# A branch projection computed by seven quarter products per pair of column blocks, and placed among the attention's projections

## The chip, the cores and the metric

The kernel runs on one core of a Trainium2 chip. The metric is the device time of one execution in microseconds (us); lower is better. A measurement is the median over several executions. One further execution was recorded by the hardware profiler, and the profile and the trace come from it.

The core has five engines that run side by side and meet through semaphores. TensorE (PE in the profile) multiplies matrices and writes its results to PSUM, eight banks of 128 x 512 float32. VectorE (DVE) and ScalarE (ACT) do elementwise work. GpSimd (POOL) and SyncE (SP) mainly issue transfers (DMA) here.

## What is computed

A decoder layer on 256 tokens of width 2048, all in float32:

```python
h = rms_norm(x, pre_norm_w)
proj = h @ w_in                       # q, k, v, z, beta, decay; mq, mk, mv, mz; gate_a, gate_b
oa = gated_delta_rule(...)            # 8 heads of 128, chunks of 64, then normed and gated
u_a = oa @ w_branch_a                 # 256 x 1024 @ 1024 x 2048
ob = moba_attention(...) * silu(mz)   # 8 heads of 128, causal
u_b = ob @ w_branch_b                 # 256 x 1024 @ 1024 x 2048
merged = sigmoid(gate_a) * u_a + sigmoid(gate_b) * u_b
x + rms_norm(merged @ w_out, post_norm_w)     # 256 x 2048 @ 2048 x 2048
```

## The kernel before

**Precision by halves.** A float32 number is held as a high and a low half of TensorE's faster float32 format. `split` (L211) makes both from a raw tile of weights: ScalarE casts the high half (L214), VectorE subtracts it from the raw tile to get the low one (L215). The pools of raw tiles, high halves and low halves have three buffers each. A product of two numbers is three matmuls: high by high, high by low, low by high.

**Projections.** `proj_n` (L347) computes 512 columns for both tiles of 128 tokens. For each 128 rows of the weights it issues six matmuls of 512 columns (three per token tile), and one split covers two such steps. `proj_t` (L329) computes 256 columns transposed, with eight steps of a 512- and a 256-column matmul per split. Weights come in raw tiles of 1 MB on SP's queue.

**The order of the work.** `ORDER` (L40) is the list of projection blocks in the order in which TensorE runs them: ga and gb are the column blocks of the two gates, mk a pair of attention heads (queries and keys, `attention`, L852), and so on. All small work is woven between the matmuls by queues of Python generators (`Queue`, L45). Each projection calls `tick` (L132) every step (in `proj_t`, every four steps), and a generator that yields a number n goes on 2n ticks later. So a tick is a place in TensorE's program. Blocks ga, gb and mk have 16 ticks each. A matmul stays in its place of the program; other engines' instructions get their order from a scheduler at build time, which takes a ready instruction that stands earlier in the program first.

**Queues that matter here.** `gq` carries the delta rule: its scores, the inverse, and `solve` (L695), which ends with `normed` (L731; tile so), then `yield OS_WAIT` and `turned_outputs` (L773; tile ot): these transpose the results and make the halves of oaT, the stationary operand of the first branch. `aq` carries, for each of two heads at a time, `attend` (L812) in four steps: scores and softmax (tile ms; VectorE L820 to L826), transposes (pp), values (po; VectorE's om, L841), transposes of the result (pt), from which halves of obT come (L849, L850). `halves` (L448) and the product with rrow (L859) finish the queries and keys.

**The branches and the end.** After the list, a loop over four column blocks (L962) computes `ua` (eight steps of `proj_n` on oaT), multiplies the gate ga by it (L965), computes `ub` on obT, multiplies gb (L968), and hands `merge` (L925) to a queue: it adds the two, transposes the sum (tile mt) and makes the halves of mT. 

The output projection then computes its first two column blocks for the first half of the rows by seven products instead of eight (the Winograd form of Strassen's scheme on 2 x 2 quarters: token tiles by halves of the 1024 rows, halves of the rows by column blocks). Sums of quarters of mT are formed by `merge` (sums_f, SH, SL), differences of weight quarters by `differences` (L917) from tiles tq that `load_quarter` (L908) fetches on POOL's queue. `product` (L986) is one product of two quarters: 12 matmuls, two splits, four ticks. Between the products stand `third(0)`, `third(1)` and `third(2)` (L1004), parts of another column block with 24 matmuls each on two splits. Two of the sums over products wait in a tile `kept` and are added at the end.

## Time and profile before

| | |
|---|---|
| median of 3 executions | 780.57 us (779.91 to 780.75) |
| the profiled execution's own time | 780.75 us |
| its span, first to last instruction | 778.8 us |
| matmuls on TensorE | 3947 |
| mean granted TensorE clock | 0.996 |
| moved by DMA | 149.24 MB, 192 GB/s on average |

How to read it: the rows of the page and of the trace give instructions as "line engine operation output<-input". A row of the chain of waits gives the start, the duration and what ran. Matmul durations overlap, so the pace is read from a stretch divided by its count. Tiles have the names of the program without their numbers: a_ua is the PSUM bank of the first branch, lo_mk a low half of mk's weights, tq a quarter for the differences.

### The profile page before, as it was taken

Reading aid. Unit: us, or ns where it says so; the run is one execution under the profiler, and the core shown is the slowest. Engines: PE = TensorE matmul, PEld = TensorE weight load, DVE = VectorE, ACT = ScalarE, POOL = GpSimd, SP = SyncE. Lnnn points to the kernel's source line nnn. Section 1 sums busy time; section 2 is a strip of 40 time slices with the busy share of each in tenths; the row PEclk is TensorE's granted clock in tenths of the full one; section 3 lists DMA queues with packets and bytes.
Section 4 is the critical chain, followed back from the end, with each engine's and each line's share of the span. In section 5 each row is a group of like instructions: output and inputs, shape, how many; then the busy total and the mean of one; then the engine's idle time right before and its main releaser. Section 6 shows DMA issues by size and latency. Waiting matters only on the chain.

```text
span 778.8 us, 10308 instructions
## 1 busy us (share of the span) xinstructions
PE 768.0 (99%) x3947; PEld 655.4 (84%) x3947; DVE 530.7 (68%) x876; ACT 412.1 (53%) x623; POOL 24.6 (3%) x47
## 2 busy tenths in 40 slices
PE   8999999999999999999999999999999999999996
PEld 7898988898888888888888888888888888888884
DVE  5787668887864898976444665555644668986673
ACT  5677665655565545455435647354454445465451
POOL 3000000010020000001100000000000000000000
PEclk9999999999999999999999999999999999999999
DMA  8576675467479555656943455555456555577442
GB/s 304 169 226 221 185 217 163 134 196 210 162 214 280 180 203 178 201 187 205 230 135 109 152 174 168 187 162 186 162 185 228 183 197 203 192 271 270 166 158 109
DMA packets 92823, 149.24 MB, mean 192 GB/s; under 512 B 3045, under 2 KB 46694, under 8 KB 92134
## 3 DMA queue, kind: packets, MB, share of 16 engines
q1 hardware_dynamic: 89958, 136.51, 54.4%
q0 software_dynamic: 2240, 11.02, 4.8%
q10 hardware_dynamic: 576, 1.05, 0.4%
q8 instruction: 31, 0.51, 0.3%
q14 instruction: 18, 0.15, 0.1%
HBM read 145.42 MB, written 3.15 MB: 191 GB/s over the span
## 4 chain that ended last, share of the span: by engine, by line
PE 95%; DVE 2%; ACT 2%; DMA 1%; issue 0%; SPq 0%; DVEq 0%
PE a_gb L140 11%; PE a_ga L140 11%; PE a_y L140 11%; PE a_k L140 6%; PE a_zg L140 6%; PE a_mq L140 6%; PE a_mk L140 6%; PE a_v L140 6%; PE a_zm L140 6%; PE a_mv L140 5%; PE a_ub L140 5%; PE a_ua L140 5%; PE a_q L140 4%; PE sv L140 2%; PE s L140 1%; PE po L140 1%
## 5 line engine op out<-in xcount | busy, mean ns | idle before, releaser
L140 PE MATMUL a_gb<-hi_gb,hT 128*128 128x512 f32 x256 | 83.2, 396 | 0.0
L140 PE MATMUL a_ga<-hi_ga,hT 128*128 128x512 f32 x256 | 80.7, 391 | 0.0
L215 DVE TENSOR_TENSOR lo_gb<-raw_gb,hi_gb 128x1024 fp32r<-128x1024 f32 x32 | 39.2, 1224 | 41.3 <-ACT hi_gb L214 41.3
L214 ACT CAST hi_gb<-raw_gb 128x1024 fp32r<-128x1024 f32 x32 | 33.7, 1052 | 49.2 <-PE a_gb L140 33.6
L140 PEld LDWEIGHTS a_ga<-hi_ga,hT 128*128 128x128 f32 x256 | 48.1, 188 | 9.9
L140 PEld LDWEIGHTS a_gb<-hi_gb,hT 128*128 128x128 f32 x256 | 48.1, 188 | 9.9
L214 ACT CAST hi_ga<-raw_ga 128x1024 fp32r<-128x1024 f32 x32 | 33.6, 1051 | 37.9 <-PE a_ga L140 28.0
L215 DVE TENSOR_TENSOR lo_ga<-raw_ga,hi_ga 128x1024 fp32r<-128x1024 f32 x32 | 39.1, 1223 | 16.6 <-ACT hi_ga L214 16.3
L140 PE MATMUL a_ga<-lo_ga,hT 128*128 128x512 f32 x128 | 49.9, 390 | 0.0
L140 PE MATMUL a_gb<-lo_gb,hT 128*128 128x512 f32 x128 | 49.8, 389 | 0.0
L140 PE MATMUL a_zg<-hi_zg,hT 128*128 128x348 f32 (+1 forms) x192 | 46.6, 322 | 0.0
L140 PE MATMUL a_mq<-hT,hi_mq 128*128 128x512 f32 x128 | 46.4, 405 | 0.0
L140 PE MATMUL a_mk<-hT,hi_mk 128*128 128x512 f32 x128 | 46.3, 403 | 0.0
L140 PE MATMUL a_y<-hi_y,mT 128*128 128x512 f32 x144 | 45.6, 390 | 0.0
L140 PE MATMUL a_v<-hT,hi_v 128*128 128x512 f32 x128 | 45.6, 399 | 0.0
L140 PE MATMUL a_q<-hT,hi_q 128*128 128x512 f32 x128 | 45.3, 395 | 0.0
L140 PE MATMUL a_ua<-hi_ua,oaT 128*128 128x512 f32 x128 | 41.8, 395 | 0.0
L140 PE MATMUL a_k<-hT,hi_k 128*128 128x512 f32 x128 | 41.1, 404 | 0.2 <-ACT hi_k L267 0.2
L140 PE MATMUL a_zm<-hi_zm,hT 128*128 128x512 f32 x128 | 40.6, 392 | 0.0
L140 PE MATMUL a_mv<-hi_mv,hT 128*128 128x512 f32 x128 | 40.1, 391 | 0.0
L140 PE MATMUL a_ub<-hi_ub,obT 128*128 128x512 f32 x128 | 40.0, 389 | 0.0
L140 PE MATMUL a_v<-hT,lo_v 128*128 128x256 f32 x128 | 35.9, 281 | 0.0
(318 smaller groups left out, 1905.0 us busy)
## 6 DMA issues: line engine op xcount, KB each, us to landing
raw_ga<-in_w_in_dram SPq DMA_DIRECT2D x16, 1024.0 KB, 5.0
raw_gb<-in_w_in_dram SPq DMA_DIRECT2D x16, 1024.0 KB, 5.1
raw_y<-in_w_out_dram SPq DMA_DIRECT2D x15, 1024.0 KB, 5.0
raw_q<-in_w_in_dram SPq DMA_DIRECT2D x8, 1024.0 KB, 5.6
raw_mv<-in_w_in_dram SPq DMA_DIRECT2D x8, 1024.0 KB, 5.1
raw_v<-in_w_in_dram SPq DMA_DIRECT2D x8, 1024.0 KB, 5.7
raw_zm<-in_w_in_dram SPq DMA_DIRECT2D x8, 1024.0 KB, 8.3
raw_mq<-in_w_in_dram SPq DMA_DIRECT2D x8, 1024.0 KB, 5.8
```

The source lines that it names most:

```text
L140: return pin(nc.tensor.matmul(*args, **kwargs))
L214: nc.scalar.copy(hi, raw)
L215: nc.vector.tensor_tensor(lo, raw, hi.bitcast(F32), op=ALU.subtract)
```

## The change

The first branch is computed for pairs of column blocks (0 and 1, then 2 and 3) by the same seven products as the output: token tile by half of oaT's rows on one side, half of the weights' rows by column block on the other. Each pair is one entry of the order, `ua0` and `ua1`; they stand before and after `mk3`. The second branch's blocks become a function `branch`: `ub0` and `ub1` stand in the order between gb1 and gb2, and blocks 2 and 3 run after the list with the merges. ga3 moves between mk1 and mk2, and gb0 and gb1 behind mk3 and ua1.

For this, the turned outputs are handled together: token tile 1 first, then tile 0, then four sums of quarters with halves of their own. The attention's queues stand still while these use all four auxiliary PSUM banks. Quarters of the first branch's weights are fetched on POOL's queue into the tiles of the delta rule and its gate as these come free; the pair's differences are spread on a queue of their own. Two rows of obT hold the fourth sum until both pairs are done.

The seven products become one function for both uses. It runs p5 first, then p1, copies c12 aside and c21 into c11 so that p2 and p6 add onto them, and adds the results in PSUM, without the tile `kept`. In the output projection two of the three parts `third` go ahead of the seven products, one stays between p6 and p2, and the differences are fetched and made after `ub1`.

```diff
+T_WAIT = 3
-OS_WAIT = 5
+OS_WAIT = 3
 ORDER = (
-    "q0 mv0 zg0 q1 kq2 kq3 zg1 v0 v1 v2 ga0 zm0 zm1 ga1 mv1 v3 ga2 ga3 mk0 mk1 gb0 mk2 gb1 mk3 gb2 gb3"
+    "q0 mv0 zg0 q1 kq2 kq3 zg1 v0 v1 v2 ga0 zm0 zm1 ga1 mv1 v3 ga2 mk0 mk1 ga3 mk2 ua0 mk3 ua1 gb0 gb1 ub0 ub1 gb2 gb3"
 ).split()
...
-        for q in (gq, vq, mq, *aq, *extra):
+        for q in (gq, vq, mq, *(() if held else aq), *extra):
             q.tick()
...
+    def fetch(tq, w, c, i):
+        rs, cs = (0, 512, 0)[i], (c + (1, 1, 0)[i]) * 512
+        nc.gpsimd.dma_start(tq[i], w[rs : rs + 512, cs : cs + 512].rearrange("(k p) c -> p k c", p=P))
+
+    def differences(tq, c, wait):
+        yield wait
+        for o, a, b in ((0, 0, 2), (1, 1, 0), (2, 1, 2)):
+            for u in range(2):
+                us = slice(2 * u, 2 * u + 2)
+                nc.vector.tensor_tensor(tq[o][:, us], tq[a][:, us], tq[b][:, us], op=ALU.subtract)
+                yield 1
+        formed.append(c)
...
+    def seven(quarter, s_, tq, w, c, banks, name, fill=lambda i: None, done=lambda b: None, more=lambda i: None):
+        c11, c12, c21, c22 = banks
+        product([s_[0]], tq[0], [c12], [True], f"{name}p5")
+        product([quarter(0, 0)], load(w, 0, c, name), [c21], [True], f"{name}p1")
+
+        s5 = tq[0][:, 0]
+        nc.scalar.copy(s5, c12)
+        nc.scalar.copy(c11, c21)
+        fill(0)
+        raw21 = load(w, 1, c, name)
+        product([s_[1]], tq[1], [c21], [False], f"{name}p6")
+        fill(1)
+        product([quarter(0, 1)], raw21, [c11], [False], f"{name}p2")
+        nc.vector.tensor_tensor(c12, c21, s5, op=ALU.add)
+        for u in range(2):
+            us = slice(2 * u, 2 * u + 2)
+            nc.vector.tensor_tensor(tq[1][:, us], raw21[:, us], tq[1][:, us], op=ALU.subtract)
+        product([s_[2]], tq[2], [c21], [False], f"{name}p7")
+        done(c11)
+        fill(2)
+        product([s_[3]], load(w, 1, c + 1, name), [c12], [False], f"{name}p3")
+        nc.vector.tensor_tensor(c22, c21, s5, op=ALU.add)
+        done(c12)
+        more(0)
+        more(2)
+        product([quarter(1, 1)], tq[1], [c21], [False], f"{name}p4")
+        more(1)
+        done(c22)
+        done(c21)
...
+    def branch_pair(i):
+        c = 2 * i
+        while not oas or c not in formed:
+            sq.tick()
+            gq.tick()
...
+        def done(b):
+            cc, t = place[id(b)]
+            nc.vector.tensor_tensor(ga[:, cc, t, :], ga[:, cc, t, :], b, op=ALU.mult)
+
+        def more(j):
+            if i == 0:
+                fetch(tua, wa, 2, j)
+
+        seven(quarters(oaT[0]), oas, tua, wa, c, (c11, c12, c21, c22), f"ua{c}", done=done, more=more)
+        pairs.append(i)
+        if i == 0:
+            sq.add(differences(tua, 2, 2))
...
-        def turned_outputs(t, oz):
...
+        def turned_outputs(ozs):
+            a = {}
+            for t in (1, 0):
+                for g in range(2):
+                    pt = aux_tile(f"ot_{t}_{g}")
+                    for hh in range(4):
+                        tr(pt[:, hh * P : (hh + 1) * P], ozs[t][:, g, hh, :], ident)
+                    a[t, g] = pt.rearrange("p (h n) -> p h n", n=P)
+                for g in range(2):
+                    ks = slice(4 * g, 4 * g + 4)
+                    halved(oT[:, ks, t * P : (t + 1) * P], oT[:, ks, S + t * P : S + (t + 1) * P], a[t, g])
+                yield 1
+            oa_f = big.tile([P, 2, 4, P], F32, tag="tv", name="oa_f")
+            x, y = (oa_f[:, i] for i in range(2))
+            nc.scalar.copy(x, a[1, 1])
+            nc.vector.tensor_tensor(a[1, 1], a[1, 0], x, op=ALU.add)
+            nc.scalar.copy(y, a[0, 0])
+            nc.vector.tensor_tensor(a[0, 0], a[1, 1], y, op=ALU.subtract)
+            nc.scalar.copy(x, a[0, 0])
+            yield 0.5
+            nc.vector.tensor_tensor(a[0, 1], a[0, 1], x, op=ALU.subtract)
+            nc.vector.tensor_tensor(a[1, 0], y, a[1, 0], op=ALU.subtract)
+            yield 0.5
+            sums = [None] * 3 + [tuple(ob_tile()[:, h, :].rearrange("p (k n) -> p k n", n=P) for h in (6, 7))]
+            for i, o, tag in ((0, (1, 1), "tt"), (1, (0, 0), "tw"), (3, (0, 1), None), (2, (1, 0), "tv")):
+                if tag:
+                    tl = big.tile([P, 2, 4, P], F32R, tag=tag, name=f"oas_{i}")
+                    sums[i] = tl[:, 0], tl[:, 1]
+                halved(*sums[i], a[o])
                 yield 0.5
+            oas.extend(sums)
...
+        obs.append(big.tile([P, H, 2 * S], F32R, tag="g0", name="obT"))
+        tg = big.tile([P, 2, 4, 512], F32, tag="g1", name="tq_g")
+        tz = big.tile([P, 4, 512], F32, tag="z2", name="tq_z")
+        tua.extend((tg[:, 0], tz, tg[:, 1]))
+        for i in (0, 2, 1):
+            fetch(tua, wa, 0, i)
+        sq.add(differences(tua, 0, T_WAIT))
         yield OS_WAIT
-        for t in range(NT):
-            yield from turned_outputs(t, ozs[t])
+        held.append(True)
+        yield from turned_outputs(ozs)
+        held.pop()
...
+    def branch(c):
+        for q in aq:
+            q.drain()
+        pb = proj_n(wb, c * 512, ob_tile(), H, f"ub{c}")
+        for t in range(NT):
+            nc.vector.tensor_tensor(gb_tile()[:, c, t, :], gb_tile()[:, c, t, :], pb[t], op=ALU.mult)
+        for t in range(NT):
+            nc.vector.tensor_tensor(ga[:, c, t, :], ga[:, c, t, :], gb_tile()[:, c, t, :], op=ALU.add)
+        if c == 1:
+            ty.extend(big.tile([P, 4, 512], F32, tag=f"z{i}", name=f"tq_{i}") for i in range(3))
+            for i in (0, 2, 1):
+                fetch(ty, wo, 0, i)
+            formed.clear()
+            sq.add(differences(ty, 0, T_WAIT))
...
-    for c in range(D // 512):
-        pa = proj_n(wa, c * 512, oaT[0], H, f"ua{c}")
-        for t in range(NT):
-            nc.vector.tensor_tensor(ga[:, c, t, :], ga[:, c, t, :], pa[t], op=ALU.mult)
-        pb = proj_n(wb, c * 512, ob_tile(), H, f"ub{c}")
-        for t in range(NT):
-            nc.vector.tensor_tensor(gb_tile()[:, c, t, :], gb_tile()[:, c, t, :], pb[t], op=ALU.mult)
-        mq.add(merge(c, 0.5 if c < 3 else 5))
...
+    mq.add(merge(0, 0.5))
+    mq.add(merge(1, 0.5))
+    branch(2)
+    mq.add(merge(2, 0.5))
+    branch(3)
+    mq.add(merge(3, 5))
...
+    third(0)
+    third(1)
+    while not formed or not summed:
         mq.tick()
+        sq.tick()
+    c11, c12, c21, c22 = (acc_tile(f"a_y{n}") for n in ("11", "12", "21", "22"))
+    seven(quarter, list(zip(SH, SL)), ty, wo, 0, (c11, c12, c21, c22), "y", fill=lambda i: third(2) if i == 1 else None)
...
-        nc.vector.tensor_tensor(late[0], late[0], late[1], op=ALU.add)
```

133 lines of the change are left out of this document (50 added, 83 removed).

## The prediction

> **What bounds the kernel now.** I read the page's first two parts, then what TensorE (PE) waited for, then the chain of waits in order of time.
>
> ```profile
> span 778.8 us, 10308 instructions
> PE 768.0 (99%) x3947; PEld 655.4 (84%) x3947; DVE 530.7 (68%) x876; ACT 412.1 (53%) x623; POOL 24.6 (3%) x47
> PEclk9999999999999999999999999999999999999999
> PE 95%; DVE 2%; ACT 2%; DMA 1%; issue 0%; SPq 0%; DVEq 0%
> ```
> ```profile
> PE hTp L143 <- DMA x<-in_x_dram: 1.7, 2, 1.1
> PE warm L140 <- DVE epst L174: 1.1, 1, 1.1
> PE a_k L140 <- ACT hi_k L267: 0.2, 1, 0.2
> ```
> ```profile
> 381.00 8.47 PE a_mq L140 x48
> ...
> 454.26 1.34 PE po L140 x12
> ...
> 457.00 0.44 PE ot L143 x4
> ...
> 468.43 0.44 PE pt L143 x4
> ...
> 473.00 1.31 PE ms L140 x8
> 474.31 11.30 PE a_mq L140 x64
> ...
> 491.26 0.66 PE pp L143 x6
> ...
> 595.01 10.93 PE a_ua L140 x48
> 605.94 10.88 PE a_ub L140 x48
> ...
> 619.55 0.44 PE mt L143 x4
> ...
> 697.39 73.75 PE a_y L140 x324
> ```
>
> TensorE is the bound: it runs at full granted clock, is 95% of the chain, and its recorded waits sum to 3.0 us, all in the start-up. One 512-column matmul takes 10.88 / 48 = 0.2267 us (0.227 below); a tick of the interleaving queues is six of them, 1.36 us, or 11.30 / 8 = 1.41 us in the transposed projections.
>
> VectorE (DVE) is second, and not evenly. The table by stages shows where it was nearly full:
>
> ```profile
> core 0: us, PE busy (x) PEld busy (x) DVE busy (x) ACT busy (x) POOL busy (x), PEclk, DMA share, GB/s
> 447.40:474.30 26.90, 26.90 (x138) 22.58 (x137) 15.70 (x22) 14.76 (x19) 0.00 (x0) 1.00 0.58 175
> 547.10:594.50 47.40, 47.40 (x224) 39.48 (x223) 24.61 (x34) 24.59 (x34) 0.75 (x1) 1.00 0.58 195
> 640.00:662.20 22.20, 22.20 (x103) 18.39 (x103) 18.76 (x24) 11.14 (x14) 0.75 (x1) 1.00 0.60 213
> 662.20:685.40 23.20, 23.09 (x106) 18.71 (x105) 21.11 (x23) 9.50 (x10) 0.00 (x0) 1.00 0.59 204
> 685.40:702.50 17.10, 17.10 (x80) 13.86 (x79) 16.50 (x18) 12.37 (x14) 0.70 (x1) 1.00 0.70 248
> ```
>
> From 640 to 702.5 it was busy 56.4 of 62.5 us. What that cost: from 595.01 to 697.39 + 73.75 = 771.14 are 176.1 us; in them lie 384 matmuls of the two branches, 372 of the output (seven products of 12, four parts `third` of 24, two blocks' later halves of 48, 96 of the last block) and 32 transposes: 756 x 0.2267 + 8 x 0.44 = 174.9. So 1.2 us were lost in the whole end, and 2/3 to 9/10 of VectorE's time in use was affordable there. The attention stage (447 to 474) used 58% of it.
>
> **The change, part by part.** I sum against the profiled execution, 780.75 us (778.8 span and 1.95 around it), the highest of the three runs, 0.18 over their median.
>
> *Removed.* The first branch took 4 blocks x 48 = 192 matmuls. By pairs it takes 2 x 7 products x 12 = 168. 24 x 0.227 = -5.44 us. The output keeps its 372; transposes are unchanged.
>
> *What a product of 12 asks.* Before, each 1024-element split fed 12 matmuls, 2.72 us. In seven() it feeds 6, 1.36 us. The costs of VectorE and ScalarE (ACT):
>
> ```profile
> 455.17 1.12 DVE L841 SCALAR_TENSOR_TENSOR om<-po,sm,zm 128x128 f32<-128x128 f32 x4
> ...
> 473.69 0.35 DVE L820 SCALAR_TENSOR_TENSOR s<-ms,qscale,mask_m 128x128 f32<-128x128 f32 x1 [1.09 <-PE ms L140]
> ...
> 474.87 0.34 DVE L820 SCALAR_TENSOR_TENSOR s<-ms,qscale,mask_m 128x128 f32<-128x128 f32 x1
> ```
> ```profile
> 640.27 1.29 DVE L928 TENSOR_TENSOR ga<-ga,gb 128x512 f32<-128x512 f32 x2
> ...
> 664.17 2.35 DVE L922 TENSOR_TENSOR tq<-tq,tq 128x1024 f32<-128x1024 f32 x2
> ...
> 686.72 2.36 DVE L215 TENSOR_TENSOR lo_yp<-tq,hi_yp 128x1024 fp32r<-128x1024 f32 x2
> ```
> ```profile
> L451 DVE TENSOR_TENSOR y_mk<-a_mk,y_mk 128x256 f32<-128x256 f32 x8 | 3.3, 418 | 0.0
> ...
> L850 DVE TENSOR_TENSOR obT<-pt,obT 128x256 fp32r<-128x256 f32 x8 | 3.0, 417 | 1.4 <-ACT obT L849 1.4
> L783 DVE SCALAR_TENSOR_TENSOR oaT<-ot,pcol,oaT 128x512 fp32r<-128x512 f32 x4 | 3.0, 748 | 0.0
> ...
> L215 DVE TENSOR_TENSOR lo_mk<-raw_mk,hi_mk 128x1024 fp32r<-128x1024 f32 x16 | 19.6, 1224 | 19.2 <-ACT hi_mk L214 19.2
> ```
> ```profile
> 687.70 0.39 PE L140 MATMUL a_y<-hi_yp,mT 128*128 128x512 f32 x1
> ...
> 688.13 0.59 ACT L1010 COPY kept<-a_y 128x512 f32<-128x512 f32 x1 [0.30 <-PE a_y L140]
> ```
>
> Two splits or differences end 2.36 us after the first starts, and the second lasts 1.224: start to start 1.13. By the same 0.09 off the mean: 512-wide adds 0.61, the scaled halves of L783 0.66, the 256-wide 0.33. A head's scores (L820 to L826) start 474.87 - 473.69 = 1.18 apart, four om take 1.12.
>
> [...]
>
> *Where it falls.* Count ticks from the end of ga2. ga3 takes 16, so the row at 381.00 is tick 16; mk0 and mk1 are 32 more, and the first ot (457.00) comes six ticks of gb0 later, at 54. Ten ticks before it, at 44, the outputs are normed (OS_WAIT = 5). Now: mk0 0 to 16, mk1 to 32, ga3 to 48, mk2 to 64, ua0 to 92 (28 ticks, since each product ticks four times), mk3 to 108, ua1 to 136. Outputs are turned from tick 50 to 60 and the first differences made from 50 to 62, both ready for ua0. aq is held for 10 ticks: pp, po, pt, ms fall on 70, 76, 84, 87, then 99, 105, 113, 116, and pp, po on 128, 134.
>
> *First stretch, ticks 50 to 92.* VectorE: 21 splits at 1.13, less two made ahead, 21.4; six differences 6.8; eight scaled halves 5.3 and four sums 2.4 of the turned outputs; raw21 less quarter, two, 2.3; c12, c22 and two done(), 2.4; halves and rrow of mk2, six, 2.0; om 1.1; obT 0.7; half of ms' 2.4, 1.2: 45.6 us. TensorE: 14 x 1.41 + 4 x 0.44 + 84 x 0.227 + 0.66 + 1.34 + 0.44 + 1.31 = 44.3; the last low half is wanted 1.1 before the end, so 43.2. Short by 2.4. Bounds: at least the bank's wait (c21 is copied to c11 between p1 and p6, which adds to that bank with nothing between: 688.13 + 0.59 + about 0.05 less 687.70 + 0.227 = 0.85), if the attention's work is put off; at most 2.4 + 0.85 and the other half of ms, 4.5. I take 3.0, nearer the floor, since the dense stretch of 640 to 702.5 lost so little.
>
> *Second stretch, ua1.* mk3 has room (8 splits, 6 differences and some 3 us, 19 of 24.6). In ua1: 12 splits 13.6, halves 1.3, raw21 2.3, adds and done() 2.4, obT 0.7, ms 2.4: 22.7, against 19.0 + 3.75 - 1.1 = 21.7. Short by 1.0. Here ms, emitted on p1's last tick, covers the copy. From 0 (obT and ms put off) to 3.0, if the raw21 pair stands ahead of p7's splits and p7 waits for 2 us of it; I take 1.5. Behind such an instruction stand all later low halves, for which TensorE waits.
>
> *The end.* seven() in y pays the same copy, 0.85; third(0) and third(1), which lay between its products, now go ahead. The differences of y leave the dense stretch for gb2 and gb3 (VectorE 24.61 of 47.4): of the 1.2 lost there I return 0.5. Late adds go, off the path. +0.4, from -0.3 to +1.5 (the end loses again all it lost and a little more).
>
> *At nothing.* ub0 and ub1 move earlier: same matmuls, under the attention's cover, since its last pt is at tick 142 and ub0 begins at 168, so the drain finds nothing. Three fetches of 1 MB on POOL's queue and one raw load fewer on SP's per pair (4 MB more in all): nothing else stands in POOL's queue there, and SP's loads keep their three buffers, only in another order. ScalarE: 14 casts at 1.05 and the copies and exponentials, some 19 of 22.8 us; behind the c11 copy, which waits for p1's end, stand p2's casts, whose buffers aren't free sooner. Without that cover it would cost like VectorE's excess.
>
> ```profile
> tq<-in_w_out_dram POOLq DMA_DIRECT2D x3, 1024.0 KB, 6.5
> ...
> hx<-in_x_dram POOLq DMA_DIRECT2D x1, 2048.0 KB, 8.3
> ```
>
> The first differences need two quarters. At the rate of hx these take 8.3 us, against six ticks, 8.3: just in time. Behind a difference that waits stand all low halves of mk2 (rival C).
>
> Sum: -5.44 + 3.0 + 1.5 + 0.4 = -0.5, so 780.2 us.
>
> **The rivals.**
>
> *A, VectorE keeps up.* The low halves go first, attention's work and done() slip into mk3 and gb0. For it: 56.4 of 62.5 us were carried with next to no loss. Against: mk2 cannot put off the halves and differences, which ua0 itself needs. -5.44 + 0.85 + 0 + 0.4 = -4.2: 776.6 us.
>
> *B, slower: VectorE's order starves TensorE.* Instructions emitted earlier (raw21 pair, ms, om) stand ahead of low halves that TensorE wants at once. The split cycle has no spare:
>
> ```profile
> 698.82 1.05 ACT L214 CAST hi_yp<-raw_y 128x1024 fp32r<-128x1024 f32 x1 [0.30 <-PE a_y L140]
> ...
> 700.18 1.06 ACT L214 CAST hi_y<-raw_y 128x1024 fp32r<-128x1024 f32 x1 [0.30 <-PE a_y L140]
> ```
>
> A buffer freed waits 0.30, is cast (1.05), subtracted (1.22): 2.6 us against two other buffers' 2.72. Price: the upper ends, -5.44 + 4.5 + 3.0 + 1.5 = +3.6: 784.3 us. The point from which it decides: 5.0 us of stalls in the two stretches take back the whole gain. Against: the lead of two splits and TensorE's own attention work give holes. [...]
>
> *C, quarters late.* If the 3 MB move at half the rate of hx, the second lands 16.6 us after its issue, 8.3 late; two splits ahead cover 5.6: +2.7, 782.9 us.
>
> **How the numbers follow.** Forecast 0.37, A 0.31, B 0.24, C 0.08. A measurement of this kernel tells 0.2% (1.56 us) from no change: 779.0 to 782.1. The forecast's own range is 778.2 to 782.4 (0.06 below, 0.02 above that band). Faster: 0.30 of A and 0.06; slower: 0.23 of B, 0.07 of C, 0.02; same 0.32. The range for 8 in 10 reaches a little past A and B: 776.2 to 785.2.
>
> **What would show it.** 24 a_ua matmuls fewer. Waits of TensorE for lo_ua and for the c11 copy: 3.0 in mk2 and ua0, 1.5 in ua1; VectorE busy there over 90%. For A: only the 0.85 copy. For B: raw21 or ms between low halves where TensorE waits. For C: VectorE idle, released by a DMA into tq. It is wrong if ua0 and ua1 last over 27 us or under 23 each, or if a stall shows outside them.

## The result and the profile after

| | before | after |
|---|---|---|
| median of 4 executions | 780.48 us (779.91 to 780.75) | 790.08 us (789.39 to 790.95) |
| ratio after / before, 95% interval | | 1.0124 (1.0107 to 1.0142) |
| span of the profiled execution | 778.8 us | 788.5 us |
| matmuls | 3947 | 3923 |
| moved by DMA | 149.24 MB | 153.44 MB |

The changed kernel is 9.6 us slower. The forecast was 780.2 us and the range 776.2 to 785.2, so the prediction was wrong, also in its sign. Two of its own signs of being wrong are there too: ua0 and ua1 last over 27 us, and a wait stands outside these stages that it didn't name (the second branch's low half, below). The 24 matmuls are gone, as forecast; TensorE lost far more time than they save. The engines' busy time, from the profile's first part:

```profile
PE 766.5 (97%) x3923; PEld 651.8 (83%) x3923; DVE 566.7 (72%) x914; ACT 427.2 (54%) x644; POOL 29.1 (4%) x53
```

Where before all recorded waits of TensorE stood in the start-up, ten kinds now stand in the list. Those inside the kernel (the columns are the sum in us, the number of times, and the longest):

```profile
PE a_ua L144 <- DVE lo_ua2p L219: 3.1, 2, 2.2
PE a_mk L144 <- DVE lo_mk L219: 2.9, 2, 2.1
PE a_ua L144 <- DVE lo_ua0p L219: 2.3, 1, 2.3
...
PE a_ub L144 <- DVE lo_ub L219: 1.2, 1, 1.2
...
PE a_ua L144 <- ACT a_ua L762: 0.7, 1, 0.7
PE a_y L144 <- ACT a_y L762: 0.7, 1, 0.7
```

All but the last two are waits for a low half that VectorE subtracts. The table by stages, cut at the first matmul of mk2, ua0, mk3, ua1 and gb0, says what each stage cost:

```profile
core 0: us, PE busy (x) PEld busy (x) DVE busy (x) ACT busy (x) POOL busy (x), PEclk, DMA share, GB/s
449.30:477.25 27.95, 25.03 (x147) 21.49 (x146) 26.30 (x39) 18.30 (x31) 0.00 (x0) 1.00 0.56 185
477.25:505.05 27.80, 24.82 (x117) 19.85 (x115) 25.67 (x39) 18.80 (x29) 2.25 (x3) 0.95 0.61 192
505.05:529.97 24.92, 24.92 (x148) 21.93 (x146) 20.19 (x23) 10.09 (x13) 0.00 (x0) 0.98 0.62 209
529.97:558.16 28.19, 25.11 (x116) 20.31 (x115) 25.40 (x39) 18.80 (x29) 1.03 (x2) 0.94 0.37 120
```

By the durations of the prediction, mk2 needs 16 x 1.41 + 4 x 0.44 = 24.3 us, ua0 and ua1 84 x 0.2267 + 0.66 + 1.34 + 0.44 + 1.31 = 22.8 each. So mk2 lost 3.6, ua0 5.0 and ua1 5.4: 14.0 us, where the forecast had 4.5 for the three. mk3 lost 0.4, the blocks from gb0 to gb3 0.7, and the end from ub2 on 3.0 (by the chain its matmuls take from 668.14 to 780.73, 112.6 us; 468 x 0.2267 and eight groups of transposes at 0.44 are 109.6), against 1.2 before. The sum is 18.1 - 1.2 - 5.4 = +11.5. The spans differ by 9.7, because this execution's start-up happened to be 1.2 us shorter (ga2's first matmul at 335.51 us, before at 336.75); 0.6 isn't accounted for.

Three things are to be seen in these rows. VectorE was busy 94%, 92% and 90% of the three stages, as the prediction's test for a shortage said. mk3, with VectorE at 81%, lost next to nothing. And in ua0 and ua1 the mean granted clock fell to 0.95 and 0.94, which no step of the prediction has.

The chain of waits shows the shortage at work: through most of ua0 it doesn't run through TensorE at all, but from one VectorE instruction to the next.

```profile
477.41 2.77 PE a_ua L144 x12
...
481.77 0.98 DVE lo_ua0p L219
482.92 1.22 DVE lo_ua0p L219
...
486.40 2.27 DVE lo_ua0p L219 x2
488.68 1.04 DVE om L988 x4
...
490.32 1.17 DVE lo_ua0p L219 x2
...
501.56 1.15 DVE lo_ua0p L219
502.75 2.50 PE a_ua L144 x5
```

What stood ahead of that last low half is in VectorE's timeline: the scores of two heads (L967 to L970, from 498.08 to 500.5), a reciprocal that waits for ScalarE, and one of done()'s products. TensorE stood from about 500.4 to 502.75 for it.

```profile
498.08 0.34 DVE L967 SCALAR_TENSOR_TENSOR s<-ms,qscale,mask_m 128x128 f32<-128x128 f32 x1
...
500.81 0.17 DVE L973 RECIPROCAL sm<-sm 128x2 f32<-128x2 f32 x1 [0.31 <-ACT s L972]
...
501.48 1.22 DVE L219 TENSOR_TENSOR lo_ua0p<-tq_z,hi_ua0p 128x1024 fp32r<-128x1024 f32 x1
```

In ua1 the scores stand so ahead of p2's low half (a wait of 0.9), and the c12 add with the raw21 pair, 2.9 us, ahead of p7's (2.2). In mk2 sums, halves and a difference stand ahead of two low halves (0.8 and 2.1). And at the first difference VectorE itself stood for a quarter:

```profile
447.27 1.23 DVE L719 TENSOR_TENSOR tq_g<-tq_g 128x1024 f32<-128x1024 f32 x1 [1.85 <-DMA tq_g<-in_w_branch_a_dram]
```

**The clock.** Behind two of the long waits the matmuls are 0.43 us apart, not 0.227. The granted clock is 0.50 from 502.53 to 505.94 us and from 546.90 to 550.32, 3.41 us each time, and 1.00 ahead of and behind both. In windows of that length:

```profile
499.12:502.53 3.41, 1.31 (x6) 0.74 (x4) 3.10 (x8) 3.41 (x10) 0.00 (x0) 1.00 1.08 377
502.53:505.94 3.41, 3.19 (x8) 2.61 (x9) 2.61 (x6) 0.67 (x2) 0.75 (x1) 0.50 0.54 153
...
543.49:546.90 3.41, 1.22 (x6) 0.72 (x5) 3.41 (x4) 1.38 (x2) 0.00 (x0) 1.00 0.18 28
546.90:550.32 3.42, 3.42 (x10) 2.65 (x9) 2.97 (x4) 1.05 (x1) 0.00 (x0) 0.50 0.78 283
...
464.98:468.40 3.42, 1.83 (x11) 1.32 (x9) 3.42 (x5) 2.50 (x4) 0.00 (x0) 1.00 0.00 0
```

A window in which TensorE was busy for 1.31 or 1.22 us (38% and 36%) is followed by one at half clock; behind the window of the wait in mk2, busy for 1.83 us (54%), the clock stayed whole. With the matmuls 0.43 us apart, the two halved windows cost about half of 3.19 and of 3.42, 3.3 us together, 0.4 of it in mk3. They begin 546.90 - 502.53 = 44.37 = 13 x 3.413 us apart.

### The profile page after: what moved, and what is told of

Same layout as the page of the kernel before. It is cut to its first block, busy times and chain, and to the rows that moved or that the text cites. A ratio compares the mean times of both kernels' runs of the same rounds, so it can differ in the third digit from the quotient of the medians.

```text
span 788.5 us, 10337 instructions
## 1 busy us (share of the span) xinstructions
PE 766.5 (97%) x3923; PEld 651.8 (83%) x3923; DVE 566.7 (72%) x914; ACT 427.2 (54%) x644; POOL 29.1 (4%) x53
## 2 busy tenths in 40 slices
DMA packets 93400, 153.44 MB, mean 195 GB/s; under 512 B 3109, under 2 KB 46758, under 8 KB 92710
## 4 chain that ended last, share of the span: by engine, by line
PE 87%; DVE 7%; ACT 3%; DMA 2%; issue 1%; SPq 0%; POOL 0%; DVEq 0%; ACTq 0%
PE a_gb L144 11%; PE a_y L144 11%; PE a_ga L144 10%; PE a_zg L144 6%; PE a_mk L144 6%; PE a_v L144 6%; PE a_k L144 6%; PE a_zm L144 6%; PE a_mv L144 5%; PE a_mq L144 4%; PE a_q L144 4%; PE a_ub L144 4%; PE a_ua L144 2%; PE sv L144 2%; DVE lo_ua0p L219 1%; PE s L144 1%
## 5 line engine op out<-in xcount | busy, mean ns | idle before, releaser
L144 PE MATMUL a_gb<-hi_gb,hT 128*128 128x512 f32 x256 | 79.4, 390 | 0.0
L144 PE MATMUL a_v<-hT,hi_v 128*128 128x512 f32 x128 | 45.6, 399 | 0.0
L144 PE MATMUL a_y<-hi_y,mT 128*128 128x512 f32 x144 | 45.6, 391 | 0.0
L144 PE MATMUL a_mk<-hT,lo_mk 128*128 128x256 f32 x128 | 36.2, 283 | 2.9 <-DVE lo_mk L219 2.9
L144 PE MATMUL a_mq<-hT,lo_mq 128*128 128x256 f32 x128 | 36.0, 281 | 0.0
```

The source lines that it names most:

```text
L144: return pin(nc.tensor.matmul(*args, **kwargs))
```

## The experiments

Theory V says: VectorE has more work in mk2, ua0 and ua1 than time, and the order of its instructions decides which low half comes late. The rivals were O (the order alone, or one instruction: the raw21 pair), C (the quarters' transfers come late), K (seven products with a split for six matmuls can't be kept dense at all), and that the moves of blocks themselves cost. Medians are given beside the kernel before as it ran with them.

### Which part costs

**e1_moves_only**: the first branch by ordinary blocks at the new places, everything computed; no sums, fetches or differences.

```diff
-        seven(quarters(oaT[0]), oas, tua, wa, c, (c11, c12, c21, c22), f"ua{c}", done=done, more=more)
+        for cc in (c, c + 1):
+            pa = proj_n(wa, cc * 512, oaT[0], H, f"ua{cc}")
+            for t in range(NT):
+                nc.vector.tensor_tensor(ga[:, cc, t, :], ga[:, cc, t, :], pa[t], op=ALU.mult)
...
```

> The first branch by ordinary blocks (192 matmuls) at the places of ua0 and ua1; no sums of the turned outputs, no quarters fetched for it, no differences; all else as changed. Theory V (VectorE has more to do in mk2, ua0 and ua1 than TensorE's time there): the 14 us lost in these three stages go and 5.4 us of matmuls come back, about 781; what stays above 780.5 is the end. Rival M (the moves themselves cost: held attention, branches spread, aux banks): 785 or more.

Measured: 782.0 us beside 780.77, ratio 1.0013 (1.0003 to 1.0022). The two waits left are ub3's 1.2 and the output's copy, 0.7. The moves between the attention's blocks cost nothing that can be seen; the end costs about 1 us.

**e2_no_differences**: the six differences and the raw21 subtraction of each pair in the first branch are left out of the computation.

```diff
-                nc.vector.tensor_tensor(tq[o][:, us], tq[a][:, us], tq[b][:, us], op=ALU.subtract)
+                if tq is not tua:
+                    nc.vector.tensor_tensor(tq[o][:, us], tq[a][:, us], tq[b][:, us], op=ALU.subtract)
...
```

> Leaves out, for the first branch alone, the six weight differences and the raw21 pair of each pair of blocks (16 VectorE instructions of 1.13 us; the quarters are still fetched, the products use them as they are). V: the shortage in mk2 and ua0 (about 7 us without the clock) and in ua1 (3.4) is smaller than the 9 us taken out of each, so the stalls and the halved clock behind them go, all but the 0.85 of the copy and some in mk2: 778 to 781. Rival L (the split cycle with three buffers sets the pace of products that take 6 matmuls per split, whatever else VectorE does): 785 to 788.

Measured: 782.2 us, ratio 1.0018 (1.0008 to 1.0027), 7.9 us less than the changed kernel, for 8 instructions of 1.13 us less in each pair, 18 us of VectorE in all. mk2 has no wait left, and the granted clock is 1.00 from 452 to 504 us (0.998 over the whole execution). VectorE's work on the differences (with its wait for their quarter) is the cause of most of the loss; what is left is waits behind the scores (1.7 in ua0, 0.9 in ua1), the copies and the end.

### What a wait by itself costs

**e12_stalls**: the kernel before, in which VectorE writes one low half of five blocks several times over.

```diff
+EXTRA = {"ga1_2_0": 4, "ga3_2_0": 5, "gb0_2_0": 4, "gb2_2_0": 5, "gb3_2_0": 6}
...
-        nc.vector.tensor_tensor(lo, raw, hi.bitcast(F32), op=ALU.subtract)
+        for _ in range(1 + EXTRA.get(name, 0)):
+            nc.vector.tensor_tensor(lo, raw, hi.bitcast(F32), op=ALU.subtract)
```

> The kernel before, with one low half in each of ga1, ga3, gb0, gb2 and gb3 computed 5, 6, 5, 6 and 7 times over (VectorE writes the same result again), so that TensorE waits once in an otherwise dense stretch. Estimates of the waits, from 1.13 us for each repeat less about 3.1 us of lead: 1.4, 2.5, 1.4, 2.5 and 3.7 us, 11.5 us in all. Theory H (a wait of about 2.2 us or more is followed by some 3 us at half the granted clock, 1.5 us of loss): behind the three longer waits the matmuls are 0.43 us apart for about 3 us, and the time is 780.7 + 11.5 + 4.5 = about 797 us. Rival (the half clock in ua0 and ua1 has another cause): matmuls 0.227 us apart right behind every wait, about 792 us.

Measured: 812.72 us beside 781.01. The waits came out longer than estimated, since I took too much lead:

```profile
PE a_gb L142 <- DVE lo_gb L218: 12.0, 3, 5.6
PE a_ga L142 <- DVE lo_ga L218: 8.9, 2, 5.1
```

That is 20.9 us of waits, but the span is 810.7 - 778.8 = 31.9 us longer. Windows of 3.41 us around four of the five waits:

```profile
295.33:298.74 3.41, 0.54 (x2) 0.48 (x3) 3.38 (x5) 0.00 (x0) 0.00 (x0) 1.00 0.00 0
298.74:302.15 3.41, 3.41 (x9) 2.65 (x8) 3.17 (x8) 0.00 (x0) 0.00 (x0) 0.50 0.82 268
...
377.25:380.66 3.41, 0.00 (x0) 0.00 (x0) 3.41 (x4) 0.85 (x1) 1.20 (x2) 1.00 0.16 42
380.66:384.07 3.41, 1.76 (x4) 1.48 (x5) 1.56 (x2) 0.00 (x0) 1.53 (x3) 0.50 0.66 180
384.07:387.49 3.42, 3.42 (x9) 2.65 (x9) 0.00 (x0) 0.04 (x1) 0.00 (x0) 0.50 0.92 281
387.49:390.90 3.41, 3.41 (x16) 2.81 (x16) 1.22 (x1) 1.62 (x2) 0.00 (x0) 1.00 0.01 3
...
578.63:582.05 3.42, 2.09 (x5) 1.71 (x6) 1.24 (x2) 0.00 (x0) 0.00 (x0) 0.50 0.26 59
582.05:585.46 3.41, 3.41 (x10) 2.73 (x10) 0.00 (x0) 0.36 (x1) 0.00 (x0) 0.50 0.65 248
609.35:612.77 3.42, 0.59 (x1) 0.50 (x2) 2.74 (x3) 0.00 (x0) 0.00 (x0) 0.50 0.00 0
```

Theory H holds in kind and not in its form. In these rows it isn't a fixed 3 us that follow a wait but one or two windows of 3.41 us. Behind the halved windows at 298.74 and 384.07, with 9 matmuls each, the clock is 1.00 again (in the changed kernel behind the one at 502.53, with 8); behind those at 380.66 and 578.63, which begin with the rest of a wait and have 4 and 5 matmuls, it is 0.50 once more. Behind the one at 609.35, with 1, the pace says the same: the 23 matmuls from 612.18 on take 7.39 us, at 0.227 they would take 5.2. So the five waits drew seven halved windows: four full of matmuls, 4 x 1.71, and three partly idle, half of 1.76, 2.09 and 0.59, 9.1 us together. 20.9 + 9.1 = 30.0 of the 31.9. The shortest wait (1.1 us, in gb0) drew none: the 24 matmuls from 478.93 on take 5.50 us, 0.229 each.

The length of a wait alone doesn't decide: in the changed kernel the clock stayed at 1.00 behind the 2.1 us in mk2 and fell behind the 2.2 in ua1. What the rows go with is how idle one window is: TensorE was busy for 0.54 us (16%) and for none of the windows at 295.33 and 377.25 here, for 38% and 36% of the two in the changed kernel, all with 0.50 behind them, and for 54% of the one in mk2. That is an estimate from these few rows.

The half clock differs between executions of one kernel: the mean granted clock of e3's four goes from 0.990 to 0.996 (793.04 to 789.78 us), e6's four have 0.994 twice and 0.998 twice. Differences of 1.7 us between two versions with such waits are within that.

### The order of VectorE's instructions

**e3_raw21_late**: the raw21 pair is emitted behind p3's matmuls instead of ahead of p7's.

```diff
         nc.vector.tensor_tensor(c12, c21, s5, op=ALU.add)
-        for u in range(2):
-            us = slice(2 * u, 2 * u + 2)
-            nc.vector.tensor_tensor(tq[1][:, us], raw21[:, us], tq[1][:, us], op=ALU.subtract)
         product([s_[2]], tq[2], [c21], [False], f"{name}p7")
...
         product([s_[3]], load(w, 1, c + 1, name), [c12], [False], f"{name}p3")
+        for u in range(2):
+            us = slice(2 * u, 2 * u + 2)
+            nc.vector.tensor_tensor(tq[1][:, us], raw21[:, us], tq[1][:, us], op=ALU.subtract)
```

> The raw21 pair of all three uses is written behind p3 instead of ahead of p7; the same work. Rival O (the order of VectorE's queue makes the stall: the pair stands ahead of p7's low halves in ua1): the 2.3 us in ua1 and the 1.6 us of halved clock behind it go, 786. V: the shortage stays and the stall moves to p4, within 1.5 us of 790.

Measured: 790.45 us, ratio 1.0132 (1.0113 to 1.0151): no gain. In ua1 the wait of 2.2 for p7 went, the one of 0.9 for p2 stayed, and two came, 1.2 for a low half of p4 and 0.8 for the c22 add. Moving one piece of work inside a stage without room only moves the wait; O with this one instruction is out.

**e6_ms_away**: the scores of heads 4 to 7 come behind ua0 and ua1 instead of into them.

```diff
-        yield A_WAIT1
+        yield {4: 4, 5: 4, 6: 9, 7: 9}.get(h, A_WAIT1)
```

> The changed kernel with the attention's scores of mk2 and mk3 (2.4 us of VectorE each, with the rest of their chains) moved out of ua0 and ua1, to ticks 92 and 136; the same work. Theory V with the order as its trigger: the stalls of 2.3 us (p4 of ua0), 0.9 and 2.2 us (p2 and p7 of ua1) shrink by 2.4 us each and the clock isn't halved behind them: 5 to 6 us less, 784 to 785. If VectorE were short by much more than these, the stalls would only move: 788 to 790.

Measured: 788.37 us beside 780.65, ratio 1.0101 (1.0086 to 1.0116), 1.7 us less than the changed kernel (the intervals just overlap), the smaller of the gains put down. ua0's wait fell from 2.3 to 0.5, ua1's from 3.1 to 1.4, but the copy into c11 now stands uncovered in both pairs (1.3 for two, before 0.7 for one): the scores' matmuls had covered it in ua1, as the prediction had said.

**e7_t_wait**: the differences begin 2 ticks later, `T_WAIT = 4`.

> T_WAIT 4 instead of 3: the first differences are written two ticks later. Rival C (VectorE stands 1.85 us for the first quarter's transfer ahead of tick 50, and mk2's stalls come from that): 1.5 to 2 us less, 788. V: what is short is work, and the same work lies closer to ua0: 790, within 1 us.

Measured: 788.86 us, ratio 1.0110 (1.0093 to 1.0127). mk2's waits fell from 2.9 to 2.0, ua0's and ua1's stayed at 2.3 and 3.1. The time is between the two put down, but it doesn't show rival C, for VectorE still stands for the first quarter as long as before:

```profile
448.22 1.23 DVE L719 TENSOR_TENSOR tq_g<-tq_g 128x1024 f32<-128x1024 f32 x1 [1.92 <-DMA tq_g<-in_w_branch_a_dram]
```

What changed is the order behind it: the fifth difference now comes after the low half that mk2 waited 2.1 us for (469.29, behind 467.49), not ahead of it. In e2, without any difference, VectorE stands at this place too (1.30 us for a cast and 1.09 for the scores), so at most a part of the 1.85 us can be put down to C; how much, no run shows.

**e4_third_between**: in the output two of the three `third` stand between the products again.

```diff
     third(0)
-    third(1)
...
-fill=lambda i: third(2) if i == 1 else None
+fill=lambda i: third(i + 1) if i < 2 else None
```

> In the output alone: third(0) ahead, third(1) between p1 and p6 where c21 is copied, third(2) between p6 and p2. The 0.85 us wait for the copy goes, nothing else changes: 789.2. If products without a part between them cost more than that in the output, 788 or less.

Measured: 789.25 us, ratio 1.0116 (1.0100 to 1.0131). The output's wait for the copy is gone, and the gain, 0.8 us, is of its size, though the two intervals overlap.

**e9_p1_first**: p1 ahead of p5, so that the copy of c21 runs under p5.

```diff
-        product([s_[0]], tq[0], [c12], [True], f"{name}p5")
         product([quarter(0, 0)], load(w, 0, c, name), [c21], [True], f"{name}p1")
+        nc.scalar.copy(c11, c21)
+        product([s_[0]], tq[0], [c12], [True], f"{name}p5")
...
         nc.scalar.copy(s5, c12)
-        nc.scalar.copy(c11, c21)
```

> The changed kernel, with p1 ahead of p5 in the seven products, so that the copy of c21 into c11 runs under p5's twelve matmuls (2.72 us) instead of standing between p1 and p6. Everything is computed. The two waits for that copy in the profile of the changed kernel are 0.83 us (ua0) and 0.82 us (the output). Theory V (VectorE short of time in ua0): the output's 0.8 us goes, ua0's is given back as a longer wait for low halves, so 789.0 to 789.5 us. Rival (the copy is a term of its own): both go, 788.4. If the copy costs nothing because it hides: 790.1.

Measured: 791.19 us, ratio 1.0138 (1.0122 to 1.0155). Both waits for the copy are gone and 0.5 us came back in ua0 (lo_ua0p 2.8 instead of 2.3) and 0.6 in the output, as a wait for lo_y. It missed even V's 789.0; the mean granted clock of its four executions is 0.992 to 0.994. A copy taken off the path is worth nothing where the next low half is late anyway.

### Taking work off VectorE

**e5_pool_differences** and **e8_all**: GpSimd makes the first branch's differences and the raw21 subtraction; e8 has the edits of e4 and e6 too.

```diff
-                nc.vector.tensor_tensor(tq[o][:, us], tq[a][:, us], tq[b][:, us], op=ALU.subtract)
+                eng = nc.gpsimd if tq is tua else nc.vector
+                eng.tensor_tensor(tq[o][:, us], tq[a][:, us], tq[b][:, us], op=ALU.subtract)
```

> The first branch's weight differences and raw21 pairs are made by GpSimd instead of VectorE; all is computed. Theory V: as with the differences left out, 781 to 783, if GpSimd needs no more than about 2.5 us for each of the 16 and doesn't slow VectorE. If the two engines hinder each other, or a difference comes late (rival: TensorE then waits for a quarter of GpSimd's), 785 or more.

> GpSimd makes the first branch's differences, the attention's scores lie outside ua0 and ua1, and third(1) and third(2) stand between the output's products. V: what stays are the copy in ua0 (0.85; in ua1 it is no longer covered, 0.85), 1.3 in ub3 and the old 1.2 less 0.8: 780.5 - 5.4 + 2.5 = 777.5, faster than both kernels.

Measured: 794.18 us (ratio 1.0173, 1.0157 to 1.0188) and 792.06 (1.0152, 1.0137 to 1.0167). Both missed by far. VectorE's and GpSimd's timelines in e5 show why:

```profile
457.01 6.58 DVE L219 TENSOR_TENSOR lo_mq<-raw_mq,hi_mq 128x1024 fp32r<-128x1024 f32 x2
463.52 3.43 DVE L219 TENSOR_TENSOR lo_mk<-raw_mk,hi_mk 128x1024 fp32r<-128x1024 f32 x1
```
```profile
449.73 4.74 POOL L720 TENSOR_TENSOR tq_g<-tq_g 128x1024 f32<-128x1024 f32 x2 [4.44 <-DMA tq_g<-in_w_branch_a_dram]
...
459.14 6.72 POOL L720 TENSOR_TENSOR tq_g<-tq_z,tq_g 128x1024 f32<-128x1024 f32 x2
```

A low half that takes VectorE 1.22 us took 3.3 to 3.4 beside GpSimd's subtraction, which itself went from 2.4 to 3.4. 3.4 is nearly the 2.4 of the one and the 1.2 of the other; that the two took turns would be an estimate from these sums, and no run shows it. VectorE was busy for 566.3 us in all, against 566.7 in the changed kernel and 549.4 in e2, so it was spared nothing, and the kernel became 4.1 us slower than with all of this work on VectorE. The scaled halves, which read PSUM, kept their pace: two in 1.41 us at 455.49, beside GpSimd, and two in 1.40 us at 466.87, behind its last row.

**e13_sums_by_dma**: transfers that add to what lies in SBUF make the sums; the signs of two quarters are turned, so that all four are sums, and C12 and C22 come out negative and are multiplied by -1 with the gate. p1 first and the scores away, as e9 and e6.

```diff
+        nc.gpsimd.dma_start(tua[0], part(0, 0), accum_op=ALU.add)
+        nc.gpsimd.dma_start(tua[1], tua[0], accum_op=ALU.add)
+        nc.gpsimd.dma_start(tua[2], part(1, 1), accum_op=ALU.add)
...
+            nc.gpsimd.dma_start(
+                tq[1],
+                w[512:1024, c * 512 : (c + 1) * 512].rearrange("(k p) c -> p k c", p=P),
+                accum_op=ALU.add,
+            )
...
-            nc.vector.tensor_tensor(a[1, 1], a[1, 0], x, op=ALU.add)
+            nc.vector.tensor_tensor(a[1, 1], x, a[1, 0], op=ALU.subtract)
```

> The changed kernel with p1 first (as e9) and the scores of heads 4 to 7 behind the pairs (as e6), and with the first branch's quarter sums made by transfers that add to what lies in SBUF, so that VectorE makes neither the six differences nor the subtraction from raw21. The signs of two quarters are turned, so that all four sums are sums; everything is computed. VectorE has by that the load of e2, 9.0 us less per pair; DMA moves 4 MB more per pair (two quarters more from DRAM, one from SBUF, and the fourth sum's). Theory V (the loss was VectorE's): only the end's waits are left, ub3 1.3 and lo_y 0.9 us, and no half clock: 780.8 - 5.4 + (2.2 - 1.2) + 0.5 = about 777 us, faster than the kernel before. Rival D (adding transfers are late, or hinder the weights' loads): TensorE waits in ua0 or ua1 for a cast that waits for a DMA, 781 us or more. Rival K (seven products can't be kept dense): 783 us or more.

Measured: 793.91 us, ratio 1.0174 (1.0160 to 1.0188): rival D. The weights' loads came late, and mk2 waited for its casts:

```profile
PE a_mk L144 <- ACT hi_mk L218: 4.3, 2, 3.7
```
```profile
raw_mk<-in_w_in_dram SPq DMA_DIRECT2D x8, 1024.0 KB, 11.7
...
raw_ua<-in_w_branch_a_dram SPq DMA_DIRECT2D x6, 1024.0 KB, 18.0
```

The last column is the median from issue to landing; in the changed kernel it is 6.2 us for raw_mk and 5.1 for raw_ua. In ua1, where TensorE waited 2.8 us, a cast stood 3.25 us for an adding transfer itself (tq_z<-tq_g, at 539.58). So this run doesn't test V: ua0 waited 0.5 us for low halves, but no more than in e6, which leaves the differences on VectorE.

### The same work in other places

**e10_less_at_once** and **e11_both**: everything on VectorE, p1 first, `T_WAIT = 4`, mk2 ahead of ga3, the differences over 18 ticks, the merge's sums 1.5 instead of 1 apart, and the attention's steps for heads 0 to 3 ahead of tick 50, the others behind the pairs; e11 leaves out the differences and the raw21 subtraction of the first branch as e2 does.

```diff
-ga2 mk0 mk1 ga3 mk2 ua0
+ga2 mk0 mk1 mk2 ga3 ua0
...
-                yield 1
-        formed.append(c)
+                yield 1.5
+            if o == 0:
+                formed.append(c)
...
-        yield A_WAIT1
+        yield (1.5, 0.5, 17, 0.5)[h // 2]
...
-        yield A_WAIT2
+        yield 3
...
```

> The changed kernel with the same work of VectorE in other places, everything computed: p1 first, mk2 ahead of ga3 (its halves fall before the turned outputs), heads 0 to 3 of the attention done before tick 50, heads 4 and 5 with scores at tick 92 and values behind ua1, heads 6 and 7 behind ua1, the differences spread over 18 ticks instead of 12 and begun one tick later, merge sums spread. So VectorE has, from tick 48 to 92, 44.0 us of work by the rows of the profile before, against 59.9 us of TensorE. Theory V (too much of VectorE's work in one place, and its order): the stalls of ua0 and ua1 shrink to under 2 us together and the half clock behind them goes, 776.5 to 778.5 us. Rival K (seven products with a split for six matmuls can't be kept dense whatever lies beside them): ua0 and ua1 stay over 25 us each, 783 us or more.

> The kernel of e10 and, as in e2, without the six differences and the subtraction of the quarter from raw21 in the first branch (left out of the computation). Theory V: if the new places are enough, this saves nothing more, 776 to 778 us, within 1 us of e10. If VectorE is still short in e10, this is 2 us or more faster than e10. Rival K: 783 us or more here too.

Measured: 792.82 us (ratio 1.0162) and 785.86 (1.0067). They settle little, for I had put the attention's steps so close that they lost time by themselves, in both kernels alike: the delta rule's last products wait for VectorE in mk2, and behind that the matmuls of e10 are slow (8 of a_mq take 2.25 us from 432.37 on, at 400.42 8 of a_mk take 1.41).

```profile
PE so L144 <- DVE oz L877: 2.5, 1, 2.5
```

What can be read: the 2.3 us of ua0 are five waits now, none over 1.0. And the differences still cost 7 us between e10 and e11 (in e10 15 matmuls of a_mk behind a wait in mk2 take 3.97 us from 456.64 on, where at 1.41 for 8 they would take 2.6), so VectorE was still short.

**e14_spread**: p1 first, the scores away, T_WAIT 4, the differences over 18 ticks (the edits of e9, e6, e7 and the second hunk of e10) and the merge's sums 1.5 instead of 1 apart; the attention's other steps and the order of blocks stay.

> The changed kernel with everything left on VectorE and only moves that each helped or did no harm by themselves: p1 first (e9), scores of heads 4 to 7 behind the pairs (e6), T_WAIT 4 (e7), and the differences over 18 ticks instead of 12 with the first product free after the first of them, the merge's sums spread. Theory V: VectorE is still short in mk2 and ua0, so part of the loss stays: 785 to 787 us, and e13 is 8 us or more faster. If the order alone was the cause (no shortage): 780 us or less, within 3 us of e13.

Measured: 786.27 us, ratio 1.0070 (1.0057 to 1.0082), as V had it; its other half, e13 being 8 us faster, failed with e13. mk2, ua0 and ua1 wait 1.9, 1.0 and 1.4 us, none longer than 1.2, and the granted clock is 1.00 in all three.

**e15_fourth_by_dma**: as e14, and one adding transfer per pair makes the fourth sum (the lines of e13 behind p6, with adding differences on VectorE), and two merges are moved in time.

```diff
-    mq.add(merge(1, 0.5))
+    mq.add(merge(1, 2))
...
-    mq.add(merge(3, 5))
+    mq.add(merge(3, 2))
...
```

> The kernel of e14, with the first branch's fourth sum made by one adding transfer per pair (1 MB, issued behind p6, where the trace of e10 shows the DMA engines idle) instead of VectorE's subtraction from raw21, signs turned as in e13, and the merges of blocks 1 and 3 begun 3 ticks later and 6 ticks earlier, away from ub3's and p7's low halves. Everything is computed. Theory V with order (each place costs what VectorE has too much there): the 1.8 and 2.2 us left in ua0 and ua1 fall to about 1 each, the end's 2.4 to about 1, so 786.3 - 3.5 = 782 to 783.5 us. If the adding transfer is late or hinders the loads (rival D): TensorE waits for a cast or for p4, 786 us or more.

Measured: 782.66 us beside 780.50, ratio 1.0026 (1.0016 to 1.0036). ua0 and ua1 wait 0.5 and 0.7, the end 0.6. One adding transfer per pair (DMA share 0.81 in ua0 and 0.65 in ua1) let no cast come late: raw_ua lands after 5.5 us, 5.2 in e14. What the transfer and what the two merges gave wasn't run apart.

**e16_mk2_first** (e15 with mk2 ahead of ga3), **e17_two_later** (e15 with four of the six differences later: by 2 x (4 - 1.5) = 5 ticks, not 4 as put down) and **e18_two_later_mk2_first** (both):

```diff
-                yield 1.5
+                yield 4 if o == 0 and u == 1 and tq is tua else 1.5
```

> The kernel of e15 with mk2 ahead of ga3, so that mk2's halves and low halves no longer share ticks 48 to 64 with the turned outputs and the first differences; the attention's waits stay as in e14. Theory V with order: the 2.2 us that e14 loses in mk2 become under 1 in ga3, so 1 to 2 us faster than e15, 780 to 782 us. Rival O (mk2 then meets the delta rule's last steps, as in e10, whose so waited 2.5 us for VectorE): no faster than e15.

> The kernel of e15 with the second and third difference (four of VectorE's six instructions) 4 ticks later, behind the turned outputs instead of among them; the products that need them come at ticks 72 and 80. Everything is computed. Theory V with order: the waits of 0.7 and 1.0 us for lo_mk in mk2 fall to under 0.5 together, nothing else grows by more than 0.5, so about 781.5 us, 1 us faster than e15. Rival (VectorE then is short in ua0): the same 1 to 2 us reappear as waits for lo_ua0p, 782.7 us or more.

> The kernel of e17 with mk2 ahead of ga3, as e16. Theory V with order: ga3's waits for low halves (1.9 and 0.6 us in e16) fall to under 1 together, 782 to 782.5 us. Rival: they stay, 784 us, since the turned outputs alone are behind them.

Measured: 784.11 us (ratio 1.0037, 1.0023 to 1.0050), 783.18 (1.0025, 1.0016 to 1.0034) and 781.51 (1.0007, 0.9998 to 1.0016). e16 has its rival's time, but not by the delta rule's last steps, which wait for nothing: ga3 waited 2.4 us for low halves. e17 won nothing, and mk2's waits stayed at 1.7; its rival's waits in ua0 didn't come either. Only both together removed the wait ahead of ua0: the turned outputs meet neither mk2's halves nor the differences. e18's stages ga3, ua0 and ua1, and its end from ub2 on:

```profile
450.27:474.04 23.77, 23.77 (x115) 19.83 (x114) 23.77 (x38) 18.48 (x32) 0.00 (x0) 1.00 0.54 188
474.04:499.26 25.22, 23.59 (x116) 18.85 (x114) 23.38 (x29) 18.70 (x23) 3.59 (x4) 1.00 0.84 242
...
522.99:547.04 24.05, 23.26 (x111) 18.16 (x109) 21.59 (x29) 17.11 (x20) 2.08 (x2) 1.00 0.64 178
...
659.29:771.13 111.84, 111.27 (x501) 90.40 (x499) 78.29 (x89) 60.49 (x78) 1.26 (x2) 1.00 0.53 188
```

In ga3 VectorE is busy for all of 23.77 us, and TensorE loses nothing: a full VectorE is no loss as long as what stands ahead of a low half is short (in ga3 each split also feeds 12 matmuls). Against 22.8, ua0 still loses 2.4 us; ua1, in which the attention's pp no longer stands, needs 22.8 - 0.66 = 22.1 and loses 1.9; the end loses 111.8 - 109.6 = 2.2, against 1.2 before. These take back 5.3 of the 5.4 us that the matmuls save. So e18 computes the whole change at the time of the kernel before, and no version here is faster than that kernel.

Rival K is out at its price: e2 and e15 are under 783 us, and ua0 and ua1 last 24.0 and 24.2 us in e15. It isn't refuted for the rest: no version kept the seven products wholly dense, and the smallest loss in one of these stages is 1.2 us (ua0 in e15, 24.0 - 22.8).

## Why the prediction was wrong, point by point

**The removed matmuls**, -5.44: right as a count; 3947 - 3923 = 24, at the pace of 0.2267 us. As time won, no version shows it: in e18, which comes back to the time of before, waits still take nearly all of it.

**The first stretch, +3.0** (bounds 0.85 to 4.5), is the step that failed. mk2 and ua0 lost 8.6 us. The reasoning was a balance of sums: 45.6 us of VectorE from tick 50 to the last low half against 43.2 of TensorE. From tick 50 (the first ot, 452.31) to the end of that low half the trace has:

```profile
452.31:502.70 50.39, 44.54 (x239) 36.91 (x237) 47.17 (x70) 34.26 (x56) 1.50 (x2) 1.00 0.55 182
```

VectorE's work was 47.2, near the estimate, but partly by luck. Scores took 3.1 us instead of 1.2 (both heads' and the end of the two before), the splits 1.5 more (20, not 19) and small instructions 0.4; against that, two of the six differences had been made ahead of tick 50 (447.27 and 449.55), 2.3 less. And VectorE also stood for 3.2 us, which the sum didn't allow, most of it in two places:

```profile
475.68 1.23 DVE L219 TENSOR_TENSOR lo_ua0p<-tq_g,hi_ua0p 128x1024 fp32r<-128x1024 f32 x1 [1.64 <-ACT hi_ua0p L218]
...
478.42 1.23 DVE L219 TENSOR_TENSOR lo_ua0p<-raw_ua,hi_ua0p 128x1024 fp32r<-128x1024 f32 x1 [0.71 <-ACT hi_ua0p L218]
```

The cast that the first of them waits for stood itself, for a buffer that TensorE had yet to free:

```profile
474.60 1.05 ACT L218 CAST hi_ua0p<-tq_g 128x1024 fp32r<-128x1024 f32 x1 [1.89 <-PE a_mk L144]
```

So VectorE can't work ahead in a quiet place for a crowded one behind it; a balance of totals takes for granted that it can. 50.4 - 43.2 = 7.2 us, and the half clock up to ua0's end, half of 505.05 - 502.75, 1.2: 8.4 of the 8.6.

I also chose 3.0 "nearer the floor, since the dense stretch of 640 to 702.5 lost so little". That analogy was the wrong row: there a split feeds 12 matmuls for much of the time, and in ga3 of e18 VectorE was denser still at no loss. (Its rows show VectorE 84 to 96% in use, more than the 2/3 to 9/10 that the prediction read from them.) The share in use alone decides nothing; what the waits show is long work ahead of the next low half.

**The second stretch, +1.5** (bounds 0 to 3.0): 5.4 us. The two instructions that the prediction named for the upper end did it, the scores (0.9) and the raw21 pair ahead of p7 (2.2). Together that is about the upper end; what lies beyond it is the window at half clock behind them, 1.7, and some 0.6 that isn't accounted for.

**The clock** is in no term and no rival. 3.3 us came of it in the profiled execution. Without it, rival B's 784.3 would still have been 2.5 us too low. One place of the kernel before could have warned, in its start-up:

```profile
4.07:7.48 3.41, 1.71 (x13) 1.42 (x14) 0.29 (x2) 0.63 (x2) 3.21 (x4) 1.00 0.96 317
7.48:10.89 3.41, 3.25 (x12) 2.60 (x12) 3.41 (x8) 2.66 (x5) 0.99 (x1) 0.50 1.01 342
```

TensorE was busy for 1.71 us (50%) of the first window, and the next ran at 0.50. The prediction took the full clock from the page's 40 slices: a slice is 19.5 us long, and one halved window in it still shows as a 9. Behind the start-up that kernel never left TensorE without work for long.

**The end, +0.4** (to +1.5): +1.8, so 0.3 beyond the bound. The copy's 0.85 was sized rightly, 0.82 lost there, and removing it gave 0.8 (e4). The differences' departure gave nothing back, for the merges, now bunched behind ub1, put eleven instructions, 6.7 us, ahead of ub3's low half, a wait of 1.2 (e1 has the same).

**At nothing**: right for the moved blocks, ub0 and ub1, ScalarE and POOL's queue (e1). **Rival C**, 2.7 us at a chance of 0.08: VectorE stood 1.85 us for the quarter, but no run shows that TensorE lost by it (e7 keeps this wait and still gains). **Rival A** is refuted. **Rival B** was the right mechanism with too small a price; its point of decision, 5.0 us of stalls in the two stretches, was passed by 9.

**The range** ended just past rival B, the sum of the terms' upper bounds. These were themselves balances of totals, so no end held the case in which VectorE stands idle in one place and is late in the next.

## What to carry to other kernels

Where a change halves the work that each prepared operand feeds, don't balance the totals of the preparing engine over a stretch: list what stands ahead of each operand in its queue, add the time for which the engine itself has to wait, and compare with the lead that the buffers give. Put long work of that engine where no operand is wanted next, and never two such pieces in one place; places and order alone gave back 3.8 of the 9.6 us (e14), and one adding transfer per pair together with two merges moved another 3.6 (e15). Price a wait of about 2 us of the matrix engine at 2 or at 3.7 us: behind waits of 2.3 and 2.2 us the changed kernel's clock was 0.50 for 3.41 us, behind one of 2.1 it was 1.00.

## What the runs showed of the hardware

- TensorE's granted clock fell to 0.50 for 3.41 us at a time: from 502.53 and from 546.90 us in the changed kernel, from 7.48 in the kernel before, from 298.74 in e12. TensorE was busy for 38%, 36%, 50% and 16% of the 3.41 us ahead of these; behind 54% (464.98 in the changed kernel) the clock was 1.00. Halved windows with 8 to 10 matmuls (502.53 and 546.90; in e12 298.74 and 384.07) were followed by 1.00, those with 4 and 5 (in e12 380.66 and 578.63) by 0.50.
- GpSimd's subtraction of 1024 float32 per partition took 2.4 us in e5 (two in 4.74), and 3.4 (two in 6.72) beside VectorE's low halves, which took 3.3 to 3.4 there (two in 6.58, one in 3.43) and 1.21 at other places (lo_ua0p from tq_g).
- Transfers of 1 MB into tq_g, adding and plain ones together, landed after 11.0 us in e13 (median), the adding ones from SBUF to SBUF after 12.6. With the DMA engines at a share of 1.07 (449 to 477 us in e13) loads on another queue landed late: raw_mk after 11.7 us, 6.2 in the changed kernel, raw_ua after 18.0, there 5.1.
- One matmul of 512 columns in the format of the halves took 0.2267 us (10.88 / 48, before); six products of 128 columns in plain float32 (po at 454.26, twelve instructions) took 1.34 us, 0.22 each.
